# Second FFN's up product: four plain feature tiles instead of five, 18 half-size ones instead of 17, and its opening in another hand-set order

## The chip, the cores and the metric

The kernel runs on one core of one Trainium2 chip. The metric is the time of one execution on the device in microseconds (us); the kernel before took 835.07 us as the median of three runs (834.91 to 835.84). The engines are PE (TensorE, matrix products), DVE (VectorE), ACT (ScalarE), POOL (GpSimd) and SP (SyncE, which here issues the loads and stores).

## The reference

One layer of a streaming encoder on x of 512 tokens by 1024 features, all in float32: a half-weighted gated FFN, a mixer (chunked attention beside trailing-mean pooling), a second half-weighted gated FFN, and a last normalisation.

```python
def rmsnorm(x, g):
    y = xf * lax.rsqrt(jnp.mean(xf * xf, axis=-1, keepdims=True) + EPS)
    return (y * g).astype(x.dtype)

def swiglu_ffn(x, w_gate, w_up, w_down):      # 1024 -> 2816 -> 1024
    return (jax.nn.silu(x @ w_gate) * (x @ w_up)) @ w_down

x = x + 0.5 * swiglu_ffn(rmsnorm(x, ffn1_norm), ...)
x = x + hybrid_mixer(rmsnorm(x, mix_norm), ...)
x = x + 0.5 * swiglu_ffn(rmsnorm(x, ffn2_norm), ...)
x = rmsnorm(x, final_norm)
```

The change touches the gate and up products of the second FFN: `x @ w_gate` and `x @ w_up`, 512 x 1024 by 1024 x 2816 each.

## The kernel before, in words

**Number format.** Every product of two float32 operands is made of three products in a rounded format. An operand is split in two: ACT rounds it to a high part (`whi`, `hhi`, `ha`), and DVE subtracts that from the operand to get the low part (`wlo`, `hlo`). `mm3` (L214 to L216) then accumulates high by high, high by low and low by high. So each weight tile that is loaded costs one pass of ACT (L154 or L531) and one of DVE (L155 or L536) before PE can use it.

**Feature tiles of the up product.** The 2816 hidden features are 22 tiles of 128. For each tile PE needs 128 gate columns and 128 up columns. There are two ways to do a tile.

- A *plain* tile multiplies all 512 tokens by all eight 128-row slices of the weights, for gate and for up: 16 calls of `mm3` with 512 columns, 48 matmuls of 128x512. DVE makes two low parts of 128x1024 for it and takes its results out with L619, L625 and L880 (128x512 each).
- A *half-size* tile treats tokens, input features and the pair gate/up as a 2 by 2 block product and does it with seven block products instead of eight (a Strassen-Winograd form): 28 calls of `mm3` with 256 columns, 84 matmuls of 128x256. It needs sums of weight blocks, which DVE makes for each tile: `sum13` (L554, L555) and `sum24` (L561, L562), four of 128x512, the low parts `wlo` of L536 (four instructions, two of them on sums), and L776, L780, L789 and L880 to take the results out. Its token blocks are the same for all tiles: they are made once, in 19 pieces (`Norm.blocks`, L409, L415, then splits into `xa`, `sa` and `ha`). A piece is started by `piece` and runs on DVE and ACT.

After a tile, `sums` (L887, L888 on DVE, for every second tile) makes what the down product needs, and `make_sums` has POOL add blocks of the down weights in DRAM (L870), two transfers a tile as `RATES` says.

**The opening of the second FFN.** Its first plain tiles are not run from a loop but from a list of tokens, `OPENING`, which `opening()` (L580) reads from left to right; PE, DVE and ACT keep that order of issue, SP's is left to a scheduler. `W i` splits a loaded weight tile, and asks for the load of the tile three further on. `B0` to `B3` are the four blocks of 24 matmuls that make the first two plain tiles together; in `B1` and `B2` PE also transposes x (L1668), ACT copies that out (L1673) and SP stores it (`x_d`). `n` are three steps of the normalisation (`rb`, the factor of each token, comes out of the third, L389). `p` starts pieces of the token blocks, `P20` is the gate product of plain tile 2, `L0` to `L3` are quarters of the last plain tile, `g`, `u` and `m` take a tile's results out (L619 with L620 on ACT, then L625 and L880, then `sums`), `F` asks for loads of half-size tiles, `h0` to `h5` make the weight parts of the first half-size tile, `O` opens tiles of the result. What is left of the last plain tile when the list ends (`u` and `m`) is done inside the first half-size tile.

**The loop of half-size tiles.** From then on a loop over n (from `PLAIN[1]` to 21) runs one half-size tile per pass, and prepares in it the weight parts of the next tile: in DVE's order `low11`, `sum13`, `sum24`, `low13`, `low24`, with the taking out of the current tile between them. PE, DVE, ACT and SP all keep the order of the code.

Of the kernel before, what the change touches and what calls it, by code (L numbers as in the profile page):

```python
# [38 lines left out]

ROOM, AHEAD_OF_PARTS, ALIGN = 1024 + 128, 16, 64  # L40
OFF_AT = 32
PLAIN = (5, 5)
RATES = [[2] * (n - 1) + [0] + [2] * (FF // P - n - 2) + [0] * 2 for n in PLAIN]
PROBS = 3
M_TILES = 16
# [14 lines left out]
ACT_FIX, DVE_FIX, QK_NORM, NORM = 0.09, 0.1, 3.7538, 3.08  # L60
AHEAD_AT = 8
OPENING = (
    "W1 n0 B0 n1 W2 n2 B1 W3 p B2 p p p p p p W4 p B3 g0 p g1 p u0 W5 u1 p m0 m1 O1 W6 W7 p p P20 P21 W8 "
    "P30 g2 p u2 m2 p P31 W9 g3 u3 m3 F0 F1 L0 h0 F2 h1 F3 L1 p h2 L2 p h3 p L3 h4 g4 h5 F4 p O0 "
)
AHEAD, NORM_AT, FILL_AT, QK_ROOT = 2, 3, 7, ()
RANKS = {
# [8 lines left out]
def layer(  # L76
# [182 lines left out]
    def constants():  # L259
        for j in range(2):  # L260
            nc.sync.dma_start(qk_sb[j * HD : (j + 1) * HD, :], qk_gain)
        nc.sync.dma_start(ps_sb, pool_scale)
        for t in range(PAD):
            nc.gpsimd.memset(inv_count[:, t : t + 1], 1.0 / (t + 1))

        flat = EXT - REL
        ext = temp()
        nc.sync.dma_start(ext[:NH, :REL], rel)
        yield
        far = temp()  # L270
        nc.vector.tensor_copy(far[:NH, :flat], ext[:NH, 0:1].to_broadcast([NH, flat]))
        nc.sync.dma_start(ext_d[:, flat:], ext[:NH, :REL])
        nc.sync.dma_start(ext_d[:, :flat], far[:NH, :flat])
        yield
# [180 lines left out]
    def ffn_up(norm, wA, down, loaded, parts=(), aside=(), further=()):  # L455
# [19 lines left out]

        plain = PLAIN[loaded]
        consts = constants()
# [1451 lines left out]
```

## Time and profile before

| what | value |
|---|---|
| runs | 835.07 us median of 3 (834.91 to 835.84) |
| the profiled execution | 835.28 us, of which the span of instructions 833.5 us |
| PE busy | 825.2 us (99% of the span), 5237 matmuls |
| DVE busy | 708.8 us (85%) |
| ACT busy | 501.7 us (60%) |
| POOL busy | 149.9 us (18%) |
| second FFN's opening, from its first matmul to the first half-size one | 501.37 to 559.24 us |

A row of the timeline gives the start, the duration, engine, line, operation, output<-inputs, shape and how many were merged; in brackets stands the idle time of that engine just before it, and what ended it. A row that stands for two instructions has their joint time. Starts of instructions that follow each other directly lie closer than the duration of one, since the engines overlap the end of one with the beginning of the next; so what an instruction costs in a full stretch is read from start to start.

### The profile page before, as it was taken

How to read it: one execution, taken by the hardware profiler on the slowest of the kernel's cores; microseconds unless marked ns; L12 is line 12 of the kernel's file. 1: busy time of each engine (PE TensorE's matmuls, PEld its weight loads, DVE VectorE, ACT ScalarE, POOL GpSimd, SP SyncE). 2: the span in 40 equal slices, each digit the busy share in tenths (PEclk: the TensorE clock that was granted, in tenths of full speed). 3: DMA queues.
4: the chain of work that ended last, by engine and by line, in shares of the span. 5: the costliest groups of instructions: out<-in, count | busy, mean ns of one | idle time of the engine just before them, and what ended most of it. 6: DMA issues, size and time to landing. Idle time of an engine off the chain costs nothing.

```text
span 833.5 us, 14248 instructions
## 1 busy us (share of the span) xinstructions
PE 825.2 (99%) x5237; PEld 738.7 (89%) x5237; DVE 708.8 (85%) x1152; ACT 501.7 (60%) x859; POOL 149.9 (18%) x212
## 2 busy tenths in 40 slices
PE   9999999999999999999999999999999999999996
PEld 8889999999988888887888888889999999988885
DVE  7999999899897678776979666989989999887896
ACT  8446555665675557558747745455566655756573
POOL 0312211222074000101111000111121121032600
PEclk9999999999999999999999999999999999999998
DMA  8667788888679973332212137757878888689922
GB/s 303 183 198 190 187 210 247 198 207 209 194 242 264 329 244 105 111 114 88 76 53 75 54 125 252 243 162 212 210 207 227 219 196 203 231 263 345 326 106 103
DMA packets 78983, 160.63 MB, mean 193 GB/s; under 512 B 7344, under 2 KB 30400, under 8 KB 78528
## 3 DMA queue, kind: packets, MB, share of 16 engines
q1 hardware_dynamic: 55824, 113.03, 39.8%
q0 software_dynamic: 22656, 46.14, 26.4%
q8 instruction: 41, 0.67, 0.3%
q10 hardware_dynamic: 432, 0.54, 0.2%
q14 instruction: 30, 0.25, 0.1%
HBM read 153.38 MB, written 50.34 MB: 244 GB/s over the span
## 4 chain that ended last, share of the span: by engine, by line
PE 96%; DVE 1%; issue 1%; DMA 1%; SPq 0%; ACT 0%; DVEq 0%
PE mm L214 23%; PE mm L216 23%; PE mm L215 23%; PE a L216 8%; PE a L214 8%; PE a L215 8%; PE a L1440 1%; PE a L1376 1%; PE a L1428 1%; DMA x<-in_xT_dram 1%; PE a L1298 0%; DVE acc L329 0%; PE a L1668 0%; DVE hlo L158 0%; PE a L333 0%
## 5 line engine op out<-in xcount | busy, mean ns | idle before, releaser
L155 DVE TENSOR_TENSOR wlo<-raw,whi 128x1024 fp32r<-128x1024 f32 (+2 forms) x115 | 124.5, 1089 | 29.5 <-ACT whi L154 29.2
L154 ACT CAST whi<-raw 128x1024 fp32r<-128x1024 f32 (+2 forms) x115 | 107.2, 943 | 48.2 <-PE mm L216 14.4
L215 PE MATMUL mm<-ha,whi 128*128 128x256 f32 x408 | 112.7, 276 | 0.0
L216 PE MATMUL mm<-ha,wlo 128*128 128x256 f32 x408 | 112.7, 276 | 0.0
L214 PE MATMUL mm<-ha,whi 128*128 128x256 f32 x408 | 112.7, 276 | 0.0
L723 ACT ACTIVATE t<-mm 128x256 f32<-128x256 f32 x102 | 39.2, 384 | 114.3 <-PE mm L216 111.7
L536 DVE TENSOR_TENSOR wlo<-wsum,whi 128x1024 fp32r<-128x1024 f32 x68 | 83.0, 1221 | 10.8 <-PE mm L216 7.9
L868 POOL COPY mark<-t 128x1 f32<-128x1 f32 x44 | 14.3, 325 | 389.0 <-DVE t L776 242.4
L214 PEld LDWEIGHTS mm<-ha,whi 128*128 128x128 f32 x408 | 76.6, 188 | 0.1
L215 PEld LDWEIGHTS mm<-ha,whi 128*128 128x128 f32 x408 | 76.6, 188 | 0.1
L216 PEld LDWEIGHTS mm<-ha,wlo 128*128 128x128 f32 x408 | 76.6, 188 | 0.0
L214 PE MATMUL mm<-hhi,whi 128*128 128x512 f32 x192 | 75.7, 397 | 0.0
L215 PE MATMUL mm<-hlo,whi 128*128 128x512 f32 x192 | 75.0, 391 | 0.0
L216 PE MATMUL mm<-hhi,wlo 128*128 128x512 f32 x192 | 74.8, 390 | 0.0
L870 POOL DMA_DIRECT2D wsum<-in_wB_dram x72 | 71.2, 1102 | 12.6 <-issue 7.2
L531 ACT CAST whi<-wsum 128x1024 fp32r<-128x1024 f32 x68 | 68.0, 1047 | 2.5 <-PE mm L215 1.5
L215 PE MATMUL mm<-wlo,ah 128*128 128x512 f32 x176 | 68.6, 390 | 0.0
L216 PE MATMUL mm<-whi,ah 128*128 128x512 f32 x176 | 68.5, 389 | 0.0
L214 PE MATMUL mm<-whi,ah 128*128 128x512 f32 x176 | 68.3, 389 | 0.0
L536 DVE TENSOR_TENSOR wlo<-raw,whi 128x512 fp32r<-128x512 f32 x68 | 62.1, 952 | 0.0
L531 ACT CAST whi<-raw 128x512 fp32r<-128x512 f32 x68 | 56.2, 827 | 2.5 <-issue 2.5
L155 DVE TENSOR_TENSOR ah<-acts,ah 128x512 fp32r<-128x512 f32 (+1 forms) x72 | 45.6, 642 | 10.9 <-ACT ah L154 8.3
(236 smaller groups left out, 2386.0 us busy)
## 6 DMA issues: line engine op xcount, KB each, us to landing
raw<-in_wA_dram SPq DMA_DIRECT2D x138, 256.0 KB, 4.1
wsum<-in_wB_dram POOLq DMA_DIRECT2D x60, 512.0 KB, 6.9
raw<-wsum SPq DMA_DIRECT2D x40, 512.0 KB, 4.8
raw<-in_wB_dram SPq DMA_DIRECT2D x30, 512.0 KB, 6.7
wsum<-wsum POOLq DMA_DIRECT2D x20, 512.0 KB, 5.5
raw<-in_wA_dram SPq DMA_DIRECT2D x18, 512.0 KB, 4.9
x<-in_xT_dram SPq DMA_DIRECT2D x16, 256.0 KB, 9.0
raw<-in_wQK_dram SPq DMA_DIRECT2D x8, 512.0 KB, 3.5
```

The source lines that it names most:

```text
L154: nc.scalar.copy(hi, src)
L155: nc.vector.tensor_tensor(lo, src, hi.bitcast(F32), op=ALU.subtract)
L214: nc.tensor.matmul(acc, a[0], b[0], start=start, stop=False, **more)
L215: nc.tensor.matmul(acc, a[0], b[1], start=False, stop=False, **more)
L216: nc.tensor.matmul(acc, a[1], b[0], start=False, stop=stop, **more)
L531: nc.scalar.copy(hi, src)
L536: nc.vector.tensor_tensor(lo, src, hi.bitcast(F32), op=ALU.subtract)
L723: nc.scalar.activation(dst, src, AF.Copy, scale=scale)
L868: nc.gpsimd.tensor_copy(mark, after[:, 0:1])
L870: nc.gpsimd.dma_start(self.rows(i, g), self.rows(self.terms[i][at], g), **(dict(accum_op=ALU.add) if at else {}),)
L1376: nc.tensor.matmul(banks[i][:, at : at + n], qT[pair][0][a][rows, t * P : (t + 1) * P], kT[pair][0][b][rows, :n], start=a + b == 0, stop=a ...
L1428: nc.tensor.transpose(tp[:, n : n + P], prob[h, t][:, j * P : (j + 1) * P], ident)
```

## The change

The second entry of `PLAIN` falls from 5 to 4. The second FFN then has four plain tiles in its opening, and its loop of half-size tiles starts at tile 4 and runs 18 times. `RATES`, which is worked out from `PLAIN`, moves its one zero with it: the tile whose evacuation starts no addition of down weights is now the fourth instead of the fifth; there are as many additions in all, in the same sequence. `OPENING` is written anew for four tiles: `W8` and `W9`, `P30` and `P31`, `u3`, `m3` and `g4` fall away, the fourth tile is now the one made in quarters, and the other tokens stand in another order. The first FFN stays with five.

```diff
-PLAIN = (5, 5)
+PLAIN = (5, 4)
 RATES = [[2] * (n - 1) + [0] + [2] * (FF // P - n - 2) + [0] * 2 for n in PLAIN]
...
 OPENING = (
-    "W1 n0 B0 n1 W2 n2 B1 W3 p B2 p p p p p p W4 p B3 g0 p g1 p u0 W5 u1 p m0 m1 O1 W6 W7 p p P20 P21 W8 "
-    "P30 g2 p u2 m2 p P31 W9 g3 u3 m3 F0 F1 L0 h0 F2 h1 F3 L1 p h2 L2 p h3 p L3 h4 g4 h5 F4 p O0 "
+    "B0 W1 n0 n1 n2 W2 p W3 p B1 p6 W4 W5 B2 p B3 g0 p2 g1 u0 u1 W6 P20 O1 p m0 p W7 P21 g2 m1 p u2 "
+    "L0 m2 L1 F0 F1 h0 F2 h1 F3 p2 h2 p L2 h3 p h4 L3 g3 h5 p O0 F4 "
 )
```

Three places show what moves. The first is DVE's order at the beginning of the opening, around the normalisation. `t` are temporaries of the normalisation, `rb` its result, `wlo` low parts of weights, and `aside` the pieces of the token blocks. Before:

```order
L384 TENSOR_SCALAR t_6110<-a_6081 128x512
L155 TENSOR_TENSOR wlo_6117<-raw_6053,whi_6116 128x1024
L386 TENSOR_TENSOR t_6112<-t_6111 128x512
L387 SCALAR_TENSOR_TENSOR t_6110<-t_6112,t_6110 128x512
L389 SCALAR_TENSOR_TENSOR rb_6124<-t_6110,t_6111 128x512
L155 TENSOR_TENSOR wlo_6183<-raw_6055,whi_6182 128x1024
L409 SCALAR_TENSOR_TENSOR aside_6050<-x_3126,gain_sb,rb_6124 128x512 x2
```

After:

```order
L384 TENSOR_SCALAR t_6110<-a_6105 128x512
L386 TENSOR_TENSOR t_6112<-t_6111 128x512
L387 SCALAR_TENSOR_TENSOR t_6110<-t_6112,t_6110 128x512
L389 SCALAR_TENSOR_TENSOR rb_6118<-t_6110,t_6111 128x512
L155 TENSOR_TENSOR wlo_6121<-raw_6053,whi_6120 128x1024
L409 SCALAR_TENSOR_TENSOR aside_6050<-x_3126,gain_sb,rb_6118 128x512
L155 TENSOR_TENSOR wlo_6128<-raw_6055,whi_6127 128x1024
```

The low part of the weights of `B2` moved from ahead of L386 to behind L389, so that the three steps that make `rb` follow each other.

The second place is DVE's order in the first half-size tile, from the taking out of the last plain tile's gate product (L619) to the second tile's last low part (the row `wlo` made from the second `wsum`). Here the numbered names differ and the rest reads alike, so only the rows around the difference stand here. Before:

```order
L880 TENSOR_TENSOR acts_6319<-mm_6487,t_6584 128x2x256
L536 TENSOR_TENSOR wlo_6627<-raw_6483,whi_6626 128x1024
L536 TENSOR_TENSOR wlo_6647<-raw_6504,whi_6646 128x512
L554 TENSOR_TENSOR wsum_6655<-raw_6504 128x512
L555 TENSOR_TENSOR wsum_6655<-raw_6504,raw_6510 128x512
```

After:

```order
L880 TENSOR_TENSOR acts_6047<-mm_6393,t_6507 128x2x256
L536 TENSOR_TENSOR wlo_6550<-raw_6428,whi_6549 128x1024
L536 TENSOR_TENSOR wlo_6570<-raw_6435,whi_6569 128x512
L887 TENSOR_TENSOR acts_6047<-acts_6047 128x256
L888 TENSOR_TENSOR acts_6047<-acts_6047 128x256
L554 TENSOR_TENSOR wsum_6580<-raw_6435 128x512
L555 TENSOR_TENSOR wsum_6580<-raw_6435,raw_6441 128x512
```

The pair L887 and L888 of the last plain tile now stands in this row of work: the last plain tile is the fourth, the second of a pair, and the fifth, which was last before, had no such pair to make.

The third place is SP's order of loads and stores while `B1` and `B2` run: `raw` from `in_wA` are weights, `x_d` the stores of the transposed x, and rows of 128x512 belong to half-size tiles. Before:

```order
L187 DMA raw_6120<-in_wA_dram 128x1024
L187 DMA raw_6186<-in_wA_dram 128x1024
L1674 DMA x_d<-t_6143 128x512
L1674 DMA x_d<-t_6151 128x512
L1674 DMA x_d<-t_6171 128x512
L1674 DMA x_d<-t_6179 128x512
L187 DMA raw_6255<-in_wA_dram 128x1024
L1674 DMA x_d<-t_6206 128x512
L1674 DMA x_d<-t_6214 128x512
L187 DMA raw_6325<-in_wA_dram 128x1024
L1674 DMA x_d<-t_6234 128x512
L1674 DMA x_d<-t_6242 128x512
```

After:

```order
L187 DMA raw_6124<-in_wA_dram 128x1024
L187 DMA raw_6131<-in_wA_dram 128x1024
L1674 DMA x_d<-t_6151 128x512
L1674 DMA x_d<-t_6159 128x512
L1674 DMA x_d<-t_6179 128x512
L1674 DMA x_d<-t_6187 128x512
L187 DMA raw_6200<-in_wA_dram 128x1024
L1674 DMA x_d<-t_6223 128x512
L1674 DMA x_d<-t_6231 128x512
L527 DMA raw_6425<-in_wA_dram 128x512 x2
L1674 DMA x_d<-t_6251 128x512
L1674 DMA x_d<-t_6259 128x512
```

The loads of the fifth plain tile are gone, and the first load of a half-size tile stands in the place of one of them, ahead of the last two stores.

## The prediction

> **What bounds the kernel now.** I read the page first (its busy shares and the chain that ended last), then stretches of the second FFN with each engine's busy time.
>
> ```profile
> span 833.5 us, 14248 instructions
> PE 825.2 (99%) x5237; PEld 738.7 (89%) x5237; DVE 708.8 (85%) x1152; ACT 501.7 (60%) x859; POOL 149.9 (18%) x212
> PE 96%; DVE 1%; issue 1%; DMA 1%; SPq 0%; ACT 0%; DVEq 0%
> ...
> core 0: us, PE busy (x) PEld busy (x) DVE busy (x) ACT busy (x) POOL busy (x), PEclk, DMA share, GB/s
> 550.00:560.00 10.00, 10.00 (x49) 8.40 (x48) 9.11 (x15) 5.82 (x9) 0.50 (x1) 1.00 0.61 210
> 579.00:588.50 9.50, 9.50 (x86) 9.50 (x85) 8.27 (x13) 5.55 (x12) 1.93 (x3) 1.00 0.78 257
> ```
>
> PE is busy for 99% of the span and is 96% of the chain. In the last 10 us of the opening, and in a whole half-size tile, it is busy throughout at the full clock (1.00), with DVE close behind (9.11 of 10, 8.27 of 9.50). A busy PE need not be at its best, so its pace is read from starts:
>
> ```profile
> 514.14 0.46 PE L214 MATMUL mm<-hhi,whi 128*128 128x512 f32 x1
> ...
> 526.60 0.39 PE L214 MATMUL mm<-hhi,whi 128*128 128x512 f32 x1
> ...
> 537.48 0.39 PE L214 MATMUL mm<-hhi,whi 128*128 128x512 f32 x1
> ...
> 559.24 0.29 PE L214 MATMUL mm<-ha,whi 128*128 128x256 f32 x1
> ...
> 571.75 0.28 PE L215 MATMUL mm<-xa,whi 128*128 128x256 f32 x1
> 571.87 0.28 PE L216 MATMUL mm<-xa,wlo 128*128 128x256 f32 x1
> ...
> 578.44 0.28 PE L214 MATMUL mm<-ha,whi 128*128 128x256 f32 x1
> ...
> 597.48 0.28 PE L214 MATMUL mm<-ha,whi 128*128 128x256 f32 x1
> ```
>
> From 526.60 to 537.48 PE starts the 48 matmuls of plain tile 2 (24 for gate, 24 for up): 10.88 us, 226.7 ns each. From 578.44 to 597.48 it does two half-size tiles, 168 matmuls: 9.52 us a tile, 113.3 ns each. Half the columns cost exactly half, so nothing but the number of streamed columns is paid in either.
>
> **The change, part by part.** *The tile itself.* 48 matmuls of 10.88 us go, 84 of 9.52 us come, all on the engine that is the path: -1.36 us. This is the whole intended effect, as long as PE stays fed. The Trainium skill, "TensorE: Matmul & The Clock Gate", section "Back-to-back issue gap", speaks against it: it gives about 81 ns a matmul sustained at 128 columns and 131 ns at 512. Drawn as a straight line to 256 columns that is an estimate of 98 ns, so 8.2 us for the half-size tile against 6.3 us for the plain one, and the change would cost 1.9 us. The spacings of 226.7 and 113.3 ns above disagree with it, and the sum goes by them.
>
> *DVE in the opening.* PE's opening becomes 10.88 us shorter. The first half-size matmul would start at 559.24 - 10.88 = 548.36. DVE's list shrinks by much less. These are its rows and waits:
>
> ```profile
> 508.26 0.69 DVE L384 TENSOR_SCALAR t<-a 128x512 f32<-128x512 f32 x1 [1.46 <-ACT t L382]
> 510.81 1.23 DVE L155 TENSOR_TENSOR wlo<-raw,whi 128x1024 fp32r<-128x1024 f32 x1 [1.85 <-ACT whi L154]
> 511.95 0.69 DVE L386 TENSOR_TENSOR t<-t 128x512 f32<-128x512 f32 x1
> 512.67 0.69 DVE L387 SCALAR_TENSOR_TENSOR t<-t,t 128x512 f32<-128x512 f32 x1
> 513.40 0.69 DVE L389 SCALAR_TENSOR_TENSOR rb<-t,t 128x512 f32<-128x512 f32 x1
> ...
> 524.11 0.75 DVE L409 SCALAR_TENSOR_TENSOR aside<-x,gain_sb,rb 128x512 f32<-128x512 f32 x1
> 524.77 0.68 DVE L619 TENSOR_TENSOR t<-mm,rb 128x512 f32<-128x512 f32 x1
> 525.38 1.22 DVE L415 TENSOR_TENSOR aside<-aside,aside 128x1024 f32<-128x1024 f32 x1
> 526.51 0.68 DVE L619 TENSOR_TENSOR t<-mm,rb 128x512 f32<-128x512 f32 x1
> ...
> DVE wlo L155 <- ACT whi L154: 4.9, 3, 2.0
> ...
> DVE acts L880 <- PE mm L216: 1.4, 1, 1.4
> DVE t L625 <- ACT t L620: 0.7, 1, 0.7
> DVE t L619 <- PE mm L216: 0.6, 1, 0.6
> ```
>
> In a full stretch a 128x1024 instruction costs 1.13 us from start to start (525.38 to 526.51), one of 128x512 about 0.60 (524.77 to 525.38), an L409 0.66. One whose input is the row before costs 0.12 more (511.95 to 512.67). The new order brings `rb` forward: L386 follows L384 at about 508.86 and L389 ends at about 511.0, 3.1 us earlier than before (513.40 + 0.69). From there to the gate L619 of the last plain tile, just before 548, I count in the new order 14 instructions of 128x1024 (15.8 us), 20 of 128x512 (12.0), eight L409 (5.3), one pair L887/L888 and the extra for dependent rows (1.2): 34.3 us of work in 37 us. It fits with 2.7 us to spare. The earliest deadline in it is kept too: the low part for `B2` ends near 511.0 + 1.2 = 512.2, and PE begins `B2` at 514.14, as before. Cost: nothing, hidden under PE, while DVE wastes less than 2.7 us. Before, it wasted 3.0 of the 4.9 us for casts behind `rb` (all but the 1.85 at 510.81), and 2.7 in the last three rows.
>
> *DVE in the first half-size tile.* Here the margin is least. Before, it reads:
>
> ```profile
> 558.76 0.69 DVE L619 TENSOR_TENSOR t<-mm,rb 128x512 f32<-128x512 f32 x1 [0.65 <-PE mm L216]
> 559.66 1.23 DVE L536 TENSOR_TENSOR wlo<-wsum,whi 128x1024 fp32r<-128x1024 f32 x1 [0.21 <-ACT whi L531]
> ...
> 563.21 1.82 DVE L536 TENSOR_TENSOR wlo<-raw,whi 128x1024 fp32r<-128x1024 f32 x2
> 564.94 0.69 DVE L554 TENSOR_TENSOR wsum<-raw 128x512 f32<-128x512 f32 x1
> ...
> 569.61 1.22 DVE L536 TENSOR_TENSOR wlo<-wsum,whi 128x1024 fp32r<-128x1024 f32 x1
> ...
> 573.08 0.42 DVE L887 TENSOR_TENSOR acts<-acts 128x256 f32<-128x256 f32 x1
> 573.54 0.42 DVE L888 TENSOR_TENSOR acts<-acts 128x256 f32<-128x256 f32 x1
> 573.88 0.69 DVE L554 TENSOR_TENSOR wsum<-raw 128x512 f32<-128x512 f32 x1
> ```
>
> DVE starts on the last plain tile's result when PE lets it (558.76, tied to PE) and works without a gap to the second tile's last `wlo`, done at 570.83. PE uses that at 571.87: 1.04 us of margin to the matmul, less to its weight load. The same chain follows PE's shift, but L887 and L888 now stand in it: 573.08 to 573.88 is 0.80 us. That leaves 0.24 to the matmul, and nothing or a little less than nothing to the weight load ahead of it, which takes 0.19 us:
>
> ```profile
> L215 PEld LDWEIGHTS mm<-ha,whi 128*128 128x128 f32 x408 | 76.6, 188 | 0.1
> ```
>
> I take 0.1 us of PE stall; the bounds are 0 and the whole pair, 0.8. It is paid once: a tile of the loop leaves DVE some idle time (8.27 busy in 9.50), which refills the margin.
>
> *ACT* loses two casts of 128x1024 and one L620 in the opening and is 5.82 of 10 busy there: nothing, hidden under PE. *POOL* has the same additions in the same sequence; one pair moves from the last plain tile into the first half-size one. It has no reader before the down product, more than 100 us on: nothing. *SP:* two loads of plain weights become four of half that size, and the load of the first half-size tile moves ahead of two stores that wait for PE's transposes. Landing times there are
>
> ```profile
> DMA to landing us min/median/max: 3.8/5.7/8.2
> ```
>
> and the shortest time the loop leaves from a load's issue to its use is that of the buffer freed by the second instruction of the row at 563.21, about 564.9, and read by L555 at about 574.5: 9.6 us, unchanged by the edit and above the longest landing of 8.2. Cost: nothing; if one comes 2 us late, 2 us.
>
> *Sum:* -10.88 + 9.52 + 0.1 = -1.26 us. The profiled execution, 833.5 us of span in 835.28, would become 832.2 in 834.0. It lies 0.2 us above the median of the runs, so the time is **833.8 us**, with a stall of 0 to 0.8 us: 833.7 to 834.5.
>
> **The rivals.** *DVE becomes the bound in the opening (the other side).* If the waits behind `rb` that cost DVE 5.7 us before (3.0 for casts, 2.7 for PE and ACT) all remain in the new order, 5.7 - 2.7 = 3.0 us more than the spare are lost, PE stalls for them, and the time is 833.8 + 3.0 = 836.8. It turns the gain into a loss once DVE wastes 1.3 us beyond the spare, and passes +0.2% at 2.9. For it: DVE was already 9.11 of 10 busy. Against: the casts of the next two weight tiles stand directly behind the table load on ACT in the new order, and 12 of the pieces need nothing but `rb` and each other, so DVE has work to put into the gaps.
>
> *The margin in the first half-size tile fails by more*: another 0.3 to 1.0 us if a cast on ACT is late as well (before, 0.21 at 559.66): 834.1 to 834.8. For it: two engines hand work to each other there. Against: ACT is little loaded.
>
> *A load lands late* through the new order of loads and stores on SP: 2 us, 835.8. Against it is the room that the first half-size load had:
>
> ```profile
> 522.43 0.88 SPq L527 DMA_DIRECT2D raw<-in_wA_dram  x2
> ...
> 546.36 0.60 ACT L531 CAST whi<-raw 128x512 fp32r<-128x512 f32 x1
> ```
>
> 24 us; the use comes 11 us earlier and the issue some 3 us, which leaves 16.
>
> *Half-size matmuls are paced by weight loads, not by columns.* If each of the 84 loads took the 0.19 us of its busy time one after another, the tile would take 16 us, 5 us more than a plain one: 840. The Trainium skill's rates above would give 837.0. Against: 85 loads went through in 9.50 us in the second stretch shown.
>
> **How the numbers follow.** The forecast (PE fed, stall 0 to 0.3) has 0.70, the failing margin 0.15, DVE as the bound 0.09, the late load 0.05, weight pacing 0.01. The runs before scatter by 0.9 us, so the forecast case spans 833.2 to 834.5; with the failing margin and the lower part of the DVE case up to 835.3 about two in ten are left out: 833.2 to 835.3. A difference of 0.2% (1.67 us) is about what a measurement can tell from none. The forecast, -1.26 us, lies inside it, and 0.4 us from its lower edge of 833.4; by the scatter I give 0.22 of the 0.70 to faster. Same: 0.48 + 0.15 + 0.03 of the late load = 0.66. Slower: 0.09 + 0.02 + 0.01 = 0.12.
>
> **What would show it right or wrong.** Right: the first half-size matmul near 548.4; PE busy in every stretch from 507 to the end of the last half-size tile, which comes 1.2 to 1.4 us earlier than before; DVE's L389 near 510.3; idle time of PE, if any, at the 15th or 27th matmul of the second half-size tile, where a `wlo` is first read, released by L536. Wrong: idle PE in `B1` to `L3` with DVE named (the DVE case), or with a DMA named (the late load), or half-size tiles apart by more than 9.52 us.

## The result and the profile after

| kernel | median | runs | beside it, before | ratio, 95% interval |
|---|---|---|---|---|
| changed | 833.23 us | 11 (832.71 to 834.64) | 835.07 us, 11 runs | 0.9978 (0.9969 to 0.9988) |
| changed, once more on another chip | 833.76 us | 11 (832.50 to 835.74) | 835.25 us, 32 runs | 0.9985 (0.9976 to 0.9993) |

The change makes the kernel faster, by 1.84 us in the first comparison and 1.49 us in the second. The profiled execution took 833.29 us.

From the page of the changed kernel: span, busy time of each engine, and the chain that ended last.

```profile
span 831.5 us, 14304 instructions
...
PE 823.8 (99%) x5273; PEld 739.2 (89%) x5273; DVE 712.1 (86%) x1159; ACT 504.1 (61%) x866; POOL 150.0 (18%) x212
...
PE 99%; DVE 0%; issue 0%; ACT 0%; DVEq 0%
```

Four stretches of the second FFN (the opening from the end of `rb` on; 10 us that hold most of the first half-size tile, which runs from 548.16 to 557.77, and the beginning of the second; most of the second; and one of the length of a later tile), each with busy us and number of instructions of PE, weight loads, DVE, ACT and POOL, then granted clock, DMA share and GB/s:

```profile
511.00:548.00 37.00, 37.00 (x179) 30.79 (x178) 34.55 (x45) 18.96 (x28) 5.41 (x9) 1.00 0.80 241
...
550.00:560.00 10.00, 10.00 (x91) 10.00 (x90) 9.93 (x17) 6.63 (x13) 1.94 (x4) 1.00 0.36 116
560.00:570.00 10.00, 10.00 (x91) 10.00 (x90) 9.86 (x15) 6.24 (x12) 2.39 (x3) 1.00 0.72 221
579.00:588.50 9.50, 9.50 (x86) 9.50 (x85) 8.27 (x13) 5.55 (x11) 1.93 (x3) 1.00 0.64 202
```

PE stays busy in all of them although DVE is now at 9.93 of 10 where the first half-size tile meets the second. The first half-size matmul and the last matmul of the kernel show what was gained. From the timeline of PE in the changed kernel:

```profile
548.16 0.29 PE L214 MATMUL mm<-ha,whi 128*128 128x256 f32 x1
...
824.54 0.28 PE L216 MATMUL a<-whi,ah 128*128 128x256 f32 x1
```

Before, in the same view, the last one was:

```profile
826.12 0.28 PE L216 MATMUL a<-whi,ah 128*128 128x256 f32 x1
```

The first half-size matmul comes 11.08 us earlier (559.24 before) and the last matmul 1.58 us earlier. Of both, 0.20 us was there before the opening's normalisation already (its L360 matmul starts at 506.81 before and at 506.61 after; the two rows below, before first), so the edit itself is worth 10.88 us at the first place and 1.38 us at the second. The rest of the difference between the two spans (833.5 and 831.5) lies ahead of the opening and behind the last matmul.

```profile
506.81 0.63 PE L360 MATMUL a<-t,ones_r 128*128 128x512 f32 x2
```

```profile
506.61 0.63 PE L360 MATMUL a<-t,ones_r 128*128 128x512 f32 x2
```

### The profile page after: what moved, and what is told of

Its sections match the earlier page's. It is cut to its first block, busy times and chain, and to the rows that moved or that the text cites. A ratio compares the mean times of both kernels' runs of the same rounds, so it can differ in the third digit from the quotient of the medians.

```text
span 831.5 us, 14304 instructions
## 1 busy us (share of the span) xinstructions
PE 823.8 (99%) x5273; PEld 739.2 (89%) x5273; DVE 712.1 (86%) x1159; ACT 504.1 (61%) x866; POOL 150.0 (18%) x212
## 4 chain that ended last, share of the span: by engine, by line
PE 99%; DVE 0%; issue 0%; ACT 0%; DVEq 0%
PE mm L214 23%; PE mm L215 23%; PE mm L216 23%; PE a L216 8%; PE a L215 8%; PE a L214 8%; PE a L1440 1%; PE a L1376 1%; PE a L1428 1%; PE a L253 0%; PE a L1298 0%; PE a L1668 0%; PE a L333 0%; PE mm L1031 0%; PE a L1031 0%; PE a L360 0%
## 5 line engine op out<-in xcount | busy, mean ns | idle before, releaser
L155 DVE TENSOR_TENSOR wlo<-raw,whi 128x1024 fp32r<-128x1024 f32 (+2 forms) x113 | 121.9, 1086 | 25.2 <-ACT whi L154 24.9
L154 ACT CAST whi<-raw 128x1024 fp32r<-128x1024 f32 (+2 forms) x113 | 104.9, 940 | 49.0 <-PE mm L216 14.4
L215 PE MATMUL mm<-ha,whi 128*128 128x256 f32 x420 | 116.0, 276 | 0.0
L216 PE MATMUL mm<-ha,wlo 128*128 128x256 f32 x420 | 116.0, 276 | 0.0
L214 PE MATMUL mm<-ha,whi 128*128 128x256 f32 x420 | 116.0, 276 | 0.0
L723 ACT ACTIVATE t<-mm 128x256 f32<-128x256 f32 x105 | 40.3, 384 | 117.4 <-PE mm L216 114.8
L536 DVE TENSOR_TENSOR wlo<-wsum,whi 128x1024 fp32r<-128x1024 f32 x70 | 85.5, 1221 | 11.3 <-ACT whi L531 6.6
L214 PEld LDWEIGHTS mm<-ha,whi 128*128 128x128 f32 x420 | 78.9, 188 | 0.1
L215 PEld LDWEIGHTS mm<-ha,whi 128*128 128x128 f32 x420 | 78.9, 188 | 0.1
L216 PEld LDWEIGHTS mm<-ha,wlo 128*128 128x128 f32 x420 | 78.9, 188 | 0.0
L214 PE MATMUL mm<-hhi,whi 128*128 128x512 f32 x176 | 69.6, 398 | 0.0
L215 PE MATMUL mm<-hlo,whi 128*128 128x512 f32 x176 | 68.9, 393 | 0.0
L216 PE MATMUL mm<-hhi,wlo 128*128 128x512 f32 x176 | 68.6, 391 | 0.0
L215 PE MATMUL mm<-wlo,ah 128*128 128x512 f32 x176 | 68.6, 390 | 0.0
L214 PE MATMUL mm<-whi,ah 128*128 128x512 f32 x176 | 68.3, 389 | 0.0
L536 DVE TENSOR_TENSOR wlo<-raw,whi 128x512 fp32r<-128x512 f32 x70 | 63.9, 952 | 0.0
L155 DVE TENSOR_TENSOR ah<-acts,ah 128x512 fp32r<-128x512 f32 (+1 forms) x72 | 45.6, 642 | 10.4 <-ACT ah L154 7.7
```

The costliest lines, as they stand in the source:

```text
L154: nc.scalar.copy(hi, src)
L155: nc.vector.tensor_tensor(lo, src, hi.bitcast(F32), op=ALU.subtract)
L214: nc.tensor.matmul(acc, a[0], b[0], start=start, stop=False, **more)
L215: nc.tensor.matmul(acc, a[0], b[1], start=False, stop=False, **more)
L216: nc.tensor.matmul(acc, a[1], b[0], start=False, stop=stop, **more)
L536: nc.vector.tensor_tensor(lo, src, hi.bitcast(F32), op=ALU.subtract)
```

## The experiments

### The order and the tile apart

*new5*: five plain tiles, but in the new order.

```diff
-PLAIN = (5, 4)
+PLAIN = (5, 5)
-    "B0 W1 n0 n1 n2 W2 p W3 p B1 p6 W4 W5 B2 p B3 g0 p2 g1 u0 u1 W6 P20 O1 p m0 p W7 P21 g2 m1 p u2 "
-    "L0 m2 L1 F0 F1 h0 F2 h1 F3 p2 h2 p L2 h3 p h4 L3 g3 h5 p O0 F4 "
+    "B0 W1 n0 n1 n2 W2 p W3 p B1 p6 W4 W5 B2 p B3 g0 p2 g1 u0 u1 W6 P20 O1 p m0 p W7 P21 g2 m1 p u2 W8 P3"
+    "0 m2 P31 W9 g3 u3 m3 L0 L1 F0 F1 h0 F2 h1 F3 p2 h2 p L2 h3 p h4 L3 g4 h5 p O0 F4"
```

> Five plain tiles as before, with the opening in the new order (the fifth tile's tokens put back). Theory: PE was fed in the old order too, so the order alone is worth nothing: the time of before, 834.8 to 835.3, first half-size matmul near 559.1. Rival, part of the measured 1.84 us comes from the order and not from the tile: 0.5 us faster than before, 834.5 or less.

Measured: 834.66 us (833.97 to 836.04, 10 runs) beside 835.24 for the kernel before; ratio 0.9995 (0.9986 to 1.0005). From L360 to the last matmul its trace takes 319.40 us, the kernel before 319.31. With five tiles the order changes nothing on PE. The median lies just below the 834.8 that was expected and above the 834.5 of the rival.

*old4*: four plain tiles, but in the old order, with the tokens of one tile taken out.

```diff
-PLAIN = (5, 5)
+PLAIN = (5, 4)
-    "... u1 p m0 m1 O1 W6 W7 p p P20 P21 W8 "
-    "P30 g2 p u2 m2 p P31 W9 g3 u3 m3 F0 F1 L0 h0 F2 h1 F3 L1 p h2 L2 p h3 p L3 h4 g4 h5 F4 p O0 "
+    "... u1 p m0 m1 O1 W6 W7 p p P20 P21 g2 "
+    "p u2 m2 p F0 F1 L0 h0 F2 h1 F3 L1 p h2 L2 p h3 p L3 h4 g3 h5 F4 p O0"
```

> Four plain tiles, with the order of before cut to four (its tokens for one tile taken out, the rest left where it stood). Theory: the gain is the tile's 1.36 us and is kept only while DVE keeps up; in the old order the token factor rb is ready 3 us later and DVE waits for casts behind it, so DVE and ACT come late to the first half-size tile and PE stalls there for 2 to 3 us: 0.6 to 1.6 us slower than before, 835.7 to 836.7. Rival, the order does not matter and the count of tiles alone sets the time: 833.2 to 833.8, as the changed kernel. First half-size matmul near 548.2 in both, since the stall comes after it.

Measured: 841.89 us in the median of 10 runs, ratio 1.0062 (1.0040 to 1.0085), but the runs are of two kinds: 835.53 and 836.16, and seven from 841.73 to 843.21 (one lies between, 838.55). The profiled execution is the shortest. In its waits of DVE those for casts are all there again (us in total, times, longest); 1.85 of the 4.9 us lie ahead of `rb`, 3.0 behind it:

```profile
DVE wlo L155 <- ACT whi L154: 4.9, 3, 2.0
```

Its timeline has L389 2.55 us later than the changed kernel has it (3.1 us later if each is counted from its own L360), and PE standing still in the first half-size tile. PE waits there for ACT, and ACT had waited for DVE just before:

```profile
512.65 0.69 DVE L389 SCALAR_TENSOR_TENSOR rb<-t,t 128x512 f32<-128x512 f32 x1
...
550.33 0.28 PE L216 MATMUL a<-xa,wlo 128*128 128x256 f32 x1
552.22 0.39 PE L214 MATMUL mm<-xa,whi 128*128 128x256 f32 x1 [1.61 <-ACT t L723]
```

```profile
549.02 1.05 ACT L531 CAST whi<-wsum 128x1024 fp32r<-128x1024 f32 x1 [1.82 <-DVE wsum L562]
550.75 0.63 ACT L620 ACTIVATE t<-t 128x512 f32<-128x512 f32 x1 [0.68 <-DVE t L619]
...
551.79 0.38 ACT L723 ACTIVATE t<-mm 128x256 f32<-128x256 f32 x1
```

From L360 to the last matmul it takes 320.57 us, 2.64 more than the changed kernel (317.93): 1.8 at the wait shown, the rest in short steps within the next 13 us. So the tile only pays with the order: the order by itself is worth nothing, and without it four tiles lose 2.6 us of PE time, more than the 1.36 they save. That explains the two short runs. The other seven are 6 us longer, which the theory did not have, and none of these seven was profiled.

### The margin in the second half-size tile

*late*: L887 and L888, whose 0.80 us cut the margin to 0.24 us, stand at the first half-size tile's last product, in DVE's order behind the second tile's last low part.

```diff
-                last_sums()
+                if n != plain or not loaded: last_sums()
                 sum13(n + 1)
...
+                if n == plain and loaded: last_sums()
                 product(acc, cut(w22, 0, S), S4, False)
```

> The kernel of the change, but the two subtractions on VectorE (L887, L888; 0.80 us) stand after the first half-size tile's last product instead of ahead of the second tile's sums, so the margin of the second tile's first matmul with the low part of the even sum grows from 0.24 us to about 1.04 us. Theory (a margin of 0.24 us is kept in every execution, no stall is paid): the same time as the change, 833.2 us, within 0.4. Rival (the small margin costs a few tenths, or is lost in some executions): 0.2 to 0.8 us less than the change, 832.4 to 833.0.

Measured: 834.45 us (834.05 to 838.70, 10 runs) beside 835.02, ratio 0.9997 (0.9985 to 1.0008). That is not the time of the change, but its profiled execution lost its time elsewhere: PE waited 0.5 us near 280 us (`PE mm L215 <- DVE wlo L155: 0.5, 1, 0.5` in the waits of PE there), and from L360 to the last matmul it takes 317.92 us, as the changed kernel does. Its second tile's `wlo` ends at 559.62 + 1.22 = 560.84 and is used at 561.88: the margin of 1.04 us is back and buys nothing on PE. It was run once more beside the changed kernel, below.

*plus1* and *plus*: the second tile's first two sums are made twice, or three times, so that DVE has 1.2 or 2.4 us more to do before the low parts.

```diff
-                last_sums()
+                last_sums(); (n == plain and loaded) and (sum13(n + 1),)
```

(*plus* has `(sum13(n + 1), sum13(n + 1))`.) Each making also takes a fresh buffer for the sum.

> The changed kernel with L554 and L555 made three times instead of once in the first half-size tile (the same sums again, 4 x 0.60 = 2.4 us more on DVE at one place). Theory: DVE's chain into the second half-size tile has 0.24 us of margin, so PE stalls about 2.2 us once, in the second half-size tile: 835.3 to 835.7, 2.0 to 2.4 slower than the changed kernel. Rival, the buffers ahead of PE hide it: 833.2, no change.

> The kernel of the change with one more making of the second half-size tile's first two sums on VectorE (two more 128x512 additions, 1.2 us): that is 1.0 us beyond the margin of 0.24 us, so TensorE should wait about 1.0 us in the second half-size tile, once. If only the wait is paid: 834.2 us. If any wait in this stream can leave TensorE at 117.8 ns a matmul for the rest of the stage (about 1400 matmuls by 4.5 ns), executions of two kinds: 834.2 and 840.4 us, with the longer one in some or most of them. If a wait has to be near 2 us for that: 834.2 in all.

Measured, *plus*: 842.11 us in the median of 8 runs, ratio 1.0068 (1.0039 to 1.0098); 835.56 as expected, 836.60 some 0.9 above that, and six from 841.62 to 844.26. *plus1*: 840.97 us, four runs from 840.20 to 841.64, ratio 1.0075 (1.0058 to 1.0091). In PE's timeline the wait of *plus1* is where the margin was; the next row is the longest wait of *plus*:

```profile
558.66 0.28 PE L215 MATMUL a<-xa,whi 128*128 128x256 f32 x1
559.68 0.38 PE L216 MATMUL a<-xa,wlo 128*128 128x256 f32 x1 [0.74 <-DVE wlo L536]
```

```profile
561.29 0.39 PE L216 MATMUL a<-xa,wlo 128*128 128x256 f32 x1 [1.49 <-DVE wlo L536]
```

The waits have the size that the margin says (about 1.0 and 2.2 us of lost starts). What follows them has not. These are the same 100 us of the half-size loop, far behind the wait, in the changed kernel, in *plus* and in *plus1*:

```profile
600.00:700.00 100.00, 100.00 (x885) 100.00 (x884) 90.83 (x139) 58.08 (x104) 19.89 (x33) 1.00 0.81 218
```

```profile
600.00:700.00 100.00, 100.00 (x852) 100.00 (x851) 88.58 (x134) 56.68 (x102) 18.03 (x30) 1.00 0.79 209
```

```profile
600.00:700.00 100.00, 100.00 (x852) 100.00 (x851) 88.58 (x134) 56.38 (x102) 18.01 (x30) 1.00 0.80 209
```

The executions of *plus*, one program, come out both near 836 and near 842 to 844, so the program and its buffers alone don't decide it. PE is busy for all of the 100 us at a granted clock of 1.00 and waits for nobody, yet it gets 852 matmuls done instead of 885: from start to start 117.8 ns instead of 113.3. The pace begins with the wait and stays to the end of the stage, about 1400 matmuls by 4.5 ns, or 6.3 us. With the 1.1 us of its waits *plus1* would be at 833.2 + 7.4 = 840.6; it is at 840.97. The groups of the same 100 us show the difference in one instruction as well: the weight load of L214 and each matmul, first in the changed kernel, then in *plus* (busy us and mean ns of one).

```profile
L214 PEld LDWEIGHTS mm<-ha,whi 128*128 128x128 f32 x128 | 24.0, 188 | 0.0
...
L214 PE MATMUL mm<-ha,whi 128*128 128x256 f32 x128 | 35.3, 276 | 0.0
```

```profile
L214 PEld LDWEIGHTS mm<-ha,whi 128*128 128x128 f32 x122 | 23.4, 192 | 0.0
...
L214 PE MATMUL mm<-ha,whi 128*128 128x256 f32 x123 | 34.6, 281 | 0.0
```

### Is it the wait that changes the pace, and where?

*work*: instead of making PE wait in the second half-size tile, it is given more to do there, the first product made three times.

```diff
-                product(acc, w11, A11, True)
+                product(acc, w11, A11, True); (n == plain + 1 and loaded) and (product(acc, w11, A11, True), product(acc, w11, A11, True))
```

> The kernel of the change, with the second half-size tile's first product (12 matmuls) made three times: 24 more matmuls by 113.3 ns = 2.7 us of TensorE work at the place where the other kernel with more VectorE work made it wait 2.2 us, and no wait. If it is the wait that brings the slower pace: 833.2 + 2.7 = 835.9 us in all executions, of one kind, at 113.3 ns. If the slower pace comes from the second tile being later by 2 us whatever the reason (transfers or engines that fall into another order): some at 842 us as well.

Measured: 836.54 us (835.94 to 838.91, 9 runs), ratio 1.0022 (1.0012 to 1.0032). No run is at 842, but only five of the nine are within 0.7 us of the 835.9 expected; the other four, up to 838.91, were not profiled. In the profiled execution PE takes 320.81 us from L360 to its last matmul, 2.88 more than the changed kernel, for 24 more matmuls (2.72), and does 885 matmuls in the 100 us from 600. Being later by as much as in *plus* does not change the pace; the wait does, or the extra work on DVE that brings it. The two were not parted: the one kernel that waits without such work is *old4*, whose longer runs have no trace.

*mid*: the extra sums are put into the eighth half-size tile, so that the wait falls into the ninth.

```diff
-                last_sums()
+                last_sums(); (n == plain + 7 and loaded) and (sum13(n + 1), sum13(n + 1), sum13(n + 1), sum13(n + 1),)
```

> The kernel of the change with four more makings of the two sums in the eighth half-size tile (4.8 us of VectorE work, of which the loop's idle time there takes up some 2.8): TensorE should wait about 2.0 us once, near 626 us, instead of in the second tile. Theory (a pause in the stream of half-size matmuls can leave it at 117.8 ns a matmul until the stage ends): executions of two kinds, 835.3 us, and 835.3 + 850 remaining matmuls by 4.5 ns = 839.1 us. Rival (the slower pace belongs to the entry of the stage, where plain and half-size tiles meet, and a pause in mid-stream is paid once): 835.3 us in all.

Measured: 838.89 us, four runs (838.83, 838.95, 840.40, and 837.01), ratio 1.0046 (1.0030 to 1.0061). The profiled execution, 838.95 us, ahead of the wait and behind it:

```profile
560.00:620.00 60.00, 60.00 (x531) 60.00 (x531) 56.24 (x86) 34.57 (x63) 11.51 (x18) 1.00 0.80 218
640.00:700.00 60.00, 60.00 (x512) 60.00 (x511) 54.07 (x83) 33.56 (x61) 11.32 (x18) 1.00 0.82 211
```

The wait itself, in its timeline of PE:

```profile
627.74 0.39 PE L216 MATMUL a<-xa,wlo 128*128 128x256 f32 x1 [1.49 <-DVE wlo L536]
```

531 matmuls in 60 us ahead of it, 512 behind it: here too the pace changes at the wait, and its price goes by the number of matmuls still to come. As in *plus* and *plus1*, PE waits at the 15th matmul of its tile, the first of the two places in a tile that the prediction named.

*first*: the same sums in the third half-size tile of the first FFN, with the wait in its fourth.

```diff
-                last_sums()
+                last_sums(); (n == plain + 2 and not loaded) and (sum13(n + 1), sum13(n + 1), sum13(n + 1), sum13(n + 1),)
```

> The kernel of the change with four more makings of the two sums in the third half-size tile of the first FFN instead of the second (4.8 us of VectorE work): TensorE should wait about 1.9 us once, near 94 us. If a pause in any stream of half-size matmuls leaves it at 117.8 ns a matmul until that stream ends: executions of two kinds, 835.1 us and 835.1 + 1140 remaining matmuls by 4.5 ns = 840.2 us, most of the longer kind, and the second FFN back at 113.3 ns. If the slower pace is a matter of the second FFN alone: 835.1 us in all.

Measured: 836.30 us in the median of 9 runs, ratio 1.0037 (1.0015 to 1.0058): five from 835.31 to 836.30, one at 837.64, three from 841.48 to 842.15. By their times both kinds appear in the first FFN too, but here the shorter one is the more frequent, which was not expected, and the longer one is some 6 us longer where 5.1 was worked out. No longer one was profiled, so that its pace is the slower one is inferred. The profiled execution is of the shorter kind: after a wait of the same 1.49 us, which ended at 94.29, its pace is back at 885 matmuls in 100 us.

```profile
100.00:200.00 100.00, 100.00 (x885) 100.00 (x884) 93.16 (x143) 60.16 (x108) 23.33 (x33) 1.00 0.87 221
```

What decides whether a wait leaves the one pace or the other was not found: it was 1.49 us in the profiled executions of *plus*, *mid* and *first*, and only the first two went on at the slower pace.

### Three plain tiles

*three*: one plain tile fewer still, in the new order.

```diff
-PLAIN = (5, 4)
+PLAIN = (5, 3)
-    "... g1 u0 u1 W6 P20 O1 p m0 p W7 P21 g2 m1 p u2 "
-    "L0 m2 L1 F0 F1 h0 F2 h1 F3 p2 h2 p L2 h3 p h4 L3 g3 h5 p O0 F4 "
+    "... g1 u0 u1 O1 p m0 p m1 p L0 L1 F0 F1 h0 F2 h1 F3 p"
+    "2 h2 p L2 h3 p h4 L3 g2 h5 p O0 F4"
```

> Three plain tiles in the new order. Theory: PE gains another 1.36 us on paper, and DVE cannot follow: 34.3 us of work less 4.1 (two low parts and three instructions of taking out) is 30.2 in a window of 37 less 10.9, 26.1: 4.1 us short, stalled for in the first half-size tile, so 2.7 us slower than the changed kernel and 0.9 to 1.5 slower than before: 836.0 to 836.6. Rival, DVE's work can be put off into the loop and each tile less is worth the same: 831.9.

Measured: 838.84 us (837.47 to 840.24, 5 runs), ratio 1.0043 (1.0029 to 1.0057), 2.2 us beyond the expected 836.0 to 836.6. DVE cannot make the token blocks in an opening shorter by another 10.88 us: it is busy for 9.91 of the 10 us, and ACT's L723, for which PE waits, stands behind casts and an activation that had waited 2.75 and 0.73 us for DVE. PE waits 3.9 us in the first half-size tile, near the 4.1 worked out, and then something else happens to it. The stretch with the wait, and PE's timeline in it:

```profile
540.00:550.00 10.00, 6.10 (x40) 5.90 (x39) 9.91 (x15) 5.09 (x9) 0.51 (x1) 0.83 0.10 34
```

```profile
540.89 0.28 PE L216 MATMUL a<-xa,wlo 128*128 128x256 f32 x1
545.07 0.58 PE L214 MATMUL mm<-xa,whi 128*128 128x256 f32 x1 [3.90 <-ACT t L723]
545.45 0.41 PE L215 MATMUL mm<-xa,whi 128*128 128x256 f32 x1
...
548.01 0.40 PE L215 MATMUL a<-ha,whi 128*128 128x256 f32 x1
548.22 0.30 PE L216 MATMUL a<-ha,wlo 128*128 128x256 f32 x1
```

After a pause of 4.2 us from start to start the matmuls are 213 ns apart (545.45 to 548.01 is twelve of them) until 548.2, and the granted clock of these 10 us is 0.83. Some 13 matmuls by 100 ns are 1.3 us, paid on top of the wait. The pauses of 1 to 2 us in the other kernels did not lower the granted clock: it is 1.00 in the 10 us around the pause in *old4* (550 to 560), *plus* (557 to 567), *plus1* (555 to 565), *mid* (620 to 630) and *first* (90 to 100). Behind its pause *three* does 885 matmuls in the 100 us from 600: the longest pause of all did not leave the slower pace in the profiled execution. The Trainium skill, "TensorE: Matmul & The Clock Gate", section "Part 1: The HAM clock gate (the "warmup" mystery)", says that an idle time of about 3.4 us brings the array's clock to half, and that start-to-start is then the columns divided by 1.2 GHz, which for 256 columns is an estimate of 213.3 ns; this trace agrees with both, at 213 ns after 4.2 us. Neither 113.3 nor 117.8 ns is the spacing that the two states of that section of the Trainium skill would give for 256 columns.

### The size of the gain

The changed kernel, *late* and *new5* were run once more, all on one chip.

> The kernel of the change itself, beside the two next ones on one chip, for the size of its gain. Its trace moved the end of TensorE's work by 1.38 us from the opening on, and 0.2 to 0.7 us more lay ahead of the opening and behind the last matmul, where the edit does nothing. If those were scatter: 1.3 us less than the kernel before, 0.9984 of it. If the new order or the shorter program also takes something from the ends: 1.8 us less, 0.9978.

> The kernel of the change with the two subtractions L887 and L888 moved behind the first half-size tile's last product, once more, now beside the kernel of the change: its profiled execution before lost 0.9 us near 280 us, 230 us ahead of the edit. Theory (the margin of 0.24 us costs nothing): the same as the change beside it, within 0.4 us. Rival (moving them costs something later in the stage, as in the median of 834.45 us before): 0.6 to 1.2 us more than the change.

> Five plain tiles in the new order once more, beside the kernel of the change. By the tile alone, 10.88 us against 9.52 us, it should take 1.36 us more than the change on the same chip. Theory (the order alone is worth nothing): the same as the kernel before, within 0.3 us. Rival (the order, or the program around it, takes 0.5 us): 834.5 us, with the change at 833.2.

| kernel | median of 11 | range | ratio to before (835.25), 95% interval |
|---|---|---|---|
| after5, the change | 833.76 us | 832.50 to 835.74 | 0.9985 (0.9976 to 0.9993) |
| late5 | 834.28 us | 833.71 to 835.46 | 0.9990 (0.9981 to 0.9999) |
| new5b, five tiles in the new order | 834.92 us | 834.32 to 836.49 | 0.9997 (0.9989 to 1.0006) |

The tile by itself, *new5b* against *after5*, is 1.16 us; 1.36 was worked out. The two sets of *late* give 0.57 and 0.97 us less than the kernel before, no better than the change: *late5* is 0.52 us above *after5*, between the 0.4 of its theory and the 0.6 of its rival, with ranges that overlap for the most part. From L360 to the last matmul the profiled executions of *late* and *late5* take 317.92 and 317.97 us, the changed kernel 317.93: on PE more margin is worth nothing as long as 0.24 us is enough, and where the 0.52 us come from, if they are more than scatter, is open. How far one execution strays shows in *after5*: its profiled one, 834.91 us, lost 1.7 us near 758 us in the down product, 210 us behind the opening, where PE waits for a split weight tile:

```profile
PE mm L215 <- DVE wlo L155: 0.8, 1, 0.8
PE mm L214 <- ACT whi L154: 0.3, 1, 0.3
```

## Why the prediction was right

*The tile* was right: 48 matmuls out and 84 in were worked out as -1.36 us, and from L360 to the last matmul the trace gives -1.38. The pace of 113.3 ns held from the third half-size tile to the 18th (9.52 us each); the first two take 9.62 and 9.58 us, in the kernel before as well, so that nothing of this falls on the change. By the estimate from the rates of the Trainium skill, "TensorE: Matmul & The Clock Gate", section "Back-to-back issue gap", the tile should have cost 1.9 us; the traces disagree with them, before and after.

*DVE in the opening* was right, and it was the step that mattered. L389 was forecast near 510.3 and starts at 510.10; the casts behind which DVE waited 4.9 us before have gone from its waits. 34.3 us of work were counted for the 37 us up to 548, and DVE is busy 34.55 us there. From the timeline of DVE in the changed kernel:

```profile
510.10 0.69 DVE L389 SCALAR_TENSOR_TENSOR rb<-t,t 128x512 f32<-128x512 f32 x1
```

Its waits from 511 to 548 us are all for PE, 2.2 us in total: DVE was ahead of PE there and never late.

```profile
DVE t L619 <- PE mm L216: 1.2, 2, 0.7
DVE acts L880 <- PE mm L216: 1.0, 1, 1.0
```

The first rival, DVE as the bound, is what *old4* is: four tiles without the earlier `rb`. PE loses 2.6 us there against the 3.0 worked out, and DVE is what it waits for in the end, so the mechanism is the one named; the new order is what keeps it away. That the size fits is in part luck, since it is made up differently: the rival had `rb` early and all 5.7 us of old waits, while *old4* has `rb` 3.1 us late and only the 3.0 us for casts, and the waits of DVE for PE and ACT at L880, L625 and L619 are gone.

*The margin in the first half-size tile* came out exactly: L536 ends at 559.32 + 1.22 = 560.54 and PE uses it at 560.78, 0.24 us later. The low part before it ends at 557.85 + 1.22 = 559.07 and is used at 559.42. The timelines of DVE and PE in the changed kernel:

```profile
557.85 1.22 DVE L536 TENSOR_TENSOR wlo<-wsum,whi 128x1024 fp32r<-128x1024 f32 x1
...
559.32 1.22 DVE L536 TENSOR_TENSOR wlo<-wsum,whi 128x1024 fp32r<-128x1024 f32 x1
...
559.42 0.28 PE L216 MATMUL a<-xa,wlo 128*128 128x256 f32 x1
...
560.78 0.28 PE L216 MATMUL mm<-xa,wlo 128*128 128x256 f32 x1
```

The stall of 0.1 us that was taken for the weight load did not come: PE's starts stay 0.11 to 0.12 us apart there. What was wrong about this step was the price of failing it. The rival "the margin fails by 0.3 to 1.0 us" was given 834.1 to 834.8, the stall alone; *plus1* fails it by 1.0 us and is at 840.97, because the pace changes too.

*ACT, POOL, SP and the loads* cost nothing, as said: PE waits for none of them between 500 and 720 us. *Weight-load pacing* by one load after another did not appear, though a milder pacing of this kind may be what the 117.8 ns is.

*The sum* of -1.26 us gave 833.8 us. The medians are 833.23 and 833.76, both within the range of 833.2 to 835.3, but the first only just: it is 0.6 us below the forecast value, and what PE gained accounts for 1.38 of its 1.84 us, so that it still lies in the range is luck. By the forecast's own limit of 0.2% the first comparison (0.22%) is the "faster" that it gave 0.22, the second (0.15%) the "same" that it gave 0.66. The 0.2 to 0.6 us beyond the sum are not in the opening, nor in PE's work behind it. They are of the size by which single executions stray at the loads near 280 and 758 us, and which of the two, a small gain there or scatter, was not settled.

## What to carry to other kernels

Shortening the bound engine's work pays only if the engine that feeds it is rid of its waits in the same stretch; here that was a matter of order, not of the tile: the same four tiles in the old order lost 2.6 us. A pause of TensorE of 1 to 2 us in a stream of short matmuls may cost far more than itself, since the stream can go on 4% more slowly until it ends, as it did in three of the five profiled executions with such a pause: so a margin of a few tenths is worth having, and a cure is to be judged over several executions, by how many of them are of the longer kind. A busy share of 100% and a granted clock of 1.00 don't show it; the number of matmuls in a fixed stretch does.

## What was not expected of the hardware

A stream of 128x256 matmuls, each with its own weight load, has two paces at the full granted clock: 113.3 ns and 117.8 ns from start to start. The second was seen in the traces of *plus*, *plus1* and *mid*, each time from a pause of PE on, and the stream kept it for up to 1400 matmuls. Of the 35 runs of the five kernels whose profiled execution loses 1.0 to 2.6 us to a pause, 23 were by their times of the longer kind, 9 of the shorter and 3 between; each kernel was profiled once. In the three traces one weight load of three takes 192 ns instead of 188. The slower pace ends with the stage: from 730 to 760 us, in the down product's matmuls of 512 columns, the profiled execution of *plus* does 134, as the changed kernel does.

```profile
730.00:760.00 30.00, 30.00 (x134) 24.82 (x134) 25.86 (x34) 19.50 (x26) 10.30 (x10) 1.00 0.84 274
```

That the weight loads, which are busy for all of the time in the half-size stream and for 24.82 of 30 us in this one, are the reason is a guess: no run took them away.
